# A transformer layer's output projection: a second of its seven block products split into seven small ones

## The chip, the cores and the metric

The kernel runs on one core of one Trainium2 chip. The metric is the device time of one execution in microseconds (us). A core has a matrix engine (TensorE, PE in the profile), three engines for elementwise work (VectorE, DVE; ScalarE, ACT; GpSimd, POOL), a queue engine (SyncE, SP) and 16 DMA engines. Each engine works through its own list of instructions in order and waits on semaphores. Transfers issued by SP and by POOL go through two queues to the same DMA engines; POOL's can add what they move to what lies at the destination.

## The reference

One layer on 512 tokens of width 2048, in float32:

```python
hn = rmsnorm(x, norm_g[i])
y = swa_mixer(hn, ...)            # windowed attention; ends with (out * silu(gate)) @ w_out
x = x + y
emb = p[i] @ ple_proj[i]
g = sigmoid(rmsnorm(x, ple_norm[i]) @ ple_gate[i])
x = x + emb * g
return rmsnorm(x, final_g)
```

The change concerns `(out * silu(gate)) @ w_out`, a product of 512x2048 with 2048x2048, and its addition to `x`.

## The kernel before

The kernel runs in stages: the first projections, attention with the gate's projection woven in (up to about 451 us of the span), the output projection (to about 600 us), the gate of the embeddings, the final norm. Every product keeps float32 accuracy from three matmuls (`mm3`, L124 to L126): each operand is split into a rounded high part and a low rest, and high x high, low x high and high x low are summed in PSUM. For the weights ACT rounds (`bhi`, L646) and DVE subtracts (`blo`, L647).

The output projection is cut into 2x2 blocks on both sides (tokens by channels, channels by outputs) and done by a scheme of Strassen's kind: seven block products instead of eight, of sums of blocks. The sums of activations (`Forms.steps`) are made by DVE; the sums of weights (`SUMS`) are made in DRAM during attention, by a copy on SP's queue and an accumulating transfer on POOL's. The products are numbered 1 to 7; product 1 is the negative one to which 6, 5 and 3 are added in the same PSUM banks.

A product has eight pieces, `(p, jj, m)`: `jj` is one of two halves of its 1024 outputs, `m` one of four parts of its 1024 channels, and each piece needs 512 KB of weights (128x1024) and makes 12 matmuls of 128x512. The list `OUT` sets the order of pieces, and for PE and SP with it the order of instructions; the other engines are ordered by a scheduler, except during attention, where the order is the written one on all engines. `Pieces` loads the weights three or four pieces ahead (`ahead`, `_prepare`) into three buffers of the tag `wraw` (`braw` in the profile) and splits them two or three ahead into three pairs `whi`, `wlo`. Between the pieces numbered `FOURTH` every fourth piece is split into a fourth pair, `spare`.

Product 4 is already made of seven small ones of the same scheme (class `Inside`), written "n" in `OUT`: 14 small pieces of 6 matmuls. Their weights stay in SBUF: product 6 loads its eight pieces into eight tiles `grown` ("seed"), and after use POOL adds another block to each of them (L703, accumulating from DRAM) and then forms the sums between tiles (L713, L723). The small pieces are woven between the pieces of product 3.

When the last piece of a half product is done, `add_y` adds it from PSUM to the one or two blocks of `x1` that need it (DVE, L1062 and L1064), or `add_in` for small products. `x1[j]` holds columns 512j to 512j+511 of x, four tiles of 128 tokens each, and is loaded from DRAM by `load_x`, four transfers of 1 MB on SP's queue, at the places `x_at`. ACT sums the squares for the next norm when a block is complete. The work of `later`, `extra` and `ahead` is given out piece by piece in the loop over `OUT`.

Of the kernel before, what the change touches and what calls it, by code (L numbers as in the profile page):

```python
# [20 lines left out]
P = 128  # L21
# [34 lines left out]
def trunk_kernel(ctx: ExitStack, tc: tile.TileContext, a: dict):  # L56
# [539 lines left out]

    SUMS = [("w_out", 7), ("w_out", 5), ("w_out", 6), ("ple_gate", 7), ("ple_gate", 5)]
    for nm, p in SUMS:
        for jj in range(2):
# [14 lines left out]
    class Pieces:  # L614
# [3 lines left out]
        def __init__(self):  # L618
            self.specs, self.base, self.made, self.grown, self.due = [], {}, {}, {}, []
            self.aside, self.first4, self.last4 = set(), 0, 0  # L620

# [3 lines left out]
        def _prepare(self, i):  # L625
# [62 lines left out]
    GROW = 4  # L688
    FOURTH = 24, 62
    FINAL_G = 6  # L690
# [3 lines left out]
    class Inside:  # L694
# [41 lines left out]
        def forms(self):  # L736
# [3 lines left out]
            for q in ORDER_IN:  # L740
# [17 lines left out]
                yield  # L758

    inside = Inside("w_out")  # L760
    SHARED = [(3, 0, 0), (3, 0, 1), "n", (3, 0, 2), "n", "n", (3, 0, 3), "n", (3, 1, 0), "n", "n", (3, 1, 1), "n", "n", (3, 1, 2), (3, 1, 3)]
    SHARED += ["n"] * (14 - SHARED.count("n"))
    OUT = [(p, jj, m) for p in (1, 7, 2, 6, 5) for jj in range(2) for m in range(4)] + SHARED

    def add_stage(nm, order):
        at = {}
        if nm == inside.nm:
            parts = [(q, i) for q in ORDER_IN for i in range(2)]
            for step in OUT:
                if step == "n":  # L770
                    B.add("part", inside, parts.pop(0))
                    continue
# [280 lines left out]
    def add_y(p, jj, tb, ps):  # L1053
# [5 lines left out]
        for (j, t), sign in whither:  # L1059
            xt = x1[j][:, t, :]  # L1060
            if sign > 0:
                nc.vector.tensor_add(xt, ps, xt)  # L1062
            else:
                nc.vector.tensor_sub(xt, xt, ps)  # L1064
            if p in (2, 5, 3, 4):
                squares(t, j)

    turns = []

# [19 lines left out]

    def inner_part():  # L1090

        x = None
        for q in ORDER_IN:
            if q in (1, 7, 2, 4):
                ps = bank(f"o4_{q}", {1: "t", 4: "t"}.get(q, "o"))
                x = ps if q == 1 else x
            else:
                ps = x
            for i in range(2):
                bh, bl = B.get(at)  # L1100
                fh, fl = inside.made[q]
                for kk in range(2):
                    k = 2 * i + kk
                    mm3(ps, fh[:, k], fl[:, k], bh[kk], bl[kk], q in (1, 7, 2, 4) and k == 0, k == 3, q in (6, 5, 3))
                if i == 1:
                    coming.append(partial_of(add_in, q, ps))
                yield

    def add_in(q, ps):
        whither = {  # L1110
# [3 lines left out]
        for (r, c), sign in whither:  # L1114
            j, t = c, 2 + r
            xt = x1[j][:, t, :]
# [7 lines left out]
    def turns_of(*v):  # L1124
        for kp, th, tag in v:
            turn(kp, th, tag)

    x_at = {(1, 1, 1): 0, (7, 0, 0): 2, (7, 0, 3): 1, (7, 1, 1): 3}
    waiting = {(7, 0): (1, 0), (2, 0): (1, 1)}
    held, coming = {}, []  # L1130
# [4 lines left out]
        (3, 0, 1): [partial_of(turn, 0, 0, "o")],  # L1135
        (3, 0, 3): [partial_of(turn, 1, 0, "o")],
        (3, 1, 0): [partial_of(turn, 2, 0, "o")],
        (3, 1, 1): [inner_forms, partial_of(turn, 3, 0, "o")], (3, 1, 2): [inner_forms], (3, 1, 3): [inner_forms],
        7: [partial_of(turn, 4, 0, "s")], 8: [partial_of(turn, 5, 0, "s"), ple_first],
# [3 lines left out]
    }  # L1143
    made, inner, seen = {}, inner_part(), 0
    ahead = {p: out_forms.steps(n) for p, n in zip((1, 7, 2, 6, 5), (7, 2, 6, 5, 3))}
    for at, step in enumerate(OUT):
        if step == "n":
            next(inner)
            step, p = seen, None
            seen += 1  # L1150
        else:
            p, jj, m = step
# [3 lines left out]
            next(made[p, jj], None)  # L1156
        for _ in range(-(-len(later) // 2)):
# [5 lines left out]
        if p in ahead:  # L1163
            next(ahead[p], None)
# [4 lines left out]
        if step == FINAL_G:  # L1169
            nc.sync.dma_start(fg, a["final_g"].partition_broadcast(P))  # L1170
    turns = []
    run(ple_first)
    assert not turns

# [295 lines left out]
```

## Time and profile before

| | |
|---|---|
| three runs | 795.31, 796.02, 797.12 us; median 796.02 |
| profiled execution | 795.63 us, its span 793.9 us |
| granted TensorE clock | 0.997 |
| DMA | 169.23 MB in the span, mean 213 GB/s |
| load of one piece, `braw<-in_w_out` | 512 KB, 4.7 us from issue to landing (median) |
| POOL's accumulating loads from w_out, 440 to 625 us | 8 of 512 KB, 11.3 us to landing (median) |

The span is measured from the first to the last instruction; the execution's own time is 1.7 us more. Busy times are summed per engine. An idle time is put down to what ended it. The DMA share is the mean busy share of the 16 DMA engines; it can read a little over 1 where packets overlap. A piece's number in the prediction is its place in `OUT`.

### The profile page before, as it was taken

What the parts mean: (1) busy time and instruction counts of PE and PEld (TensorE: products, weight loads), DVE (VectorE), ACT (ScalarE), POOL (GpSimd) and SP (SyncE); (2) the same over time, 40 slices, a digit from 0 to 9 for tenths busy, and PEclk for the clock granted to TensorE, in tenths of its full rate; (3) what the DMA queues carried; (4) which work ended last, traced back from release to release, by engine and by line L of the source; (5) the groups of instructions that cost most, each with busy time, mean ns of one, the idle gap of its engine ahead of it and who ended that gap; (6) DMA issues with size and microseconds to landing.
All of it is one profiled execution on the core that took longest, in us unless ns stands there. A gap on an engine that the chain in (4) does not pass through costs nothing.

```text
span 793.9 us, 11140 instructions
## 1 busy us (share of the span) xinstructions
PE 783.2 (99%) x3750; PEld 653.7 (82%) x3750; DVE 604.5 (76%) x1034; ACT 488.7 (62%) x999; POOL 156.9 (20%) x372
## 2 busy tenths in 40 slices
PE   9999999999999999999999999999999999999995
PEld 7888888888888888888888878888888888888884
DVE  4536478888877788687887889776888757899885
ACT  5632376677556766566666654654779756667754
POOL 0003013443243314333133200031100120200000
PEclk9999999999999999999999999999999999999998
DMA  8790585979677967889585569899973996885533
GB/s 337 275 221 8 189 239 164 249 212 252 184 224 194 228 192 201 210 225 263 151 222 130 150 217 355 330 254 303 272 218 99 358 222 218 166 217 194 170 107 106
DMA packets 45513, 169.23 MB, mean 213 GB/s; under 512 B 6464, under 2 KB 7104, under 8 KB 41616
## 3 DMA queue, kind: packets, MB, share of 16 engines
q1 hardware_dynamic: 36896, 129.01, 47.9%
q0 software_dynamic: 8272, 39.12, 26.2%
q8 instruction: 29, 0.48, 0.2%
q10 hardware_dynamic: 288, 0.39, 0.2%
q14 instruction: 28, 0.23, 0.1%
HBM read 157.44 MB, written 46.19 MB: 256 GB/s over the span
## 4 chain that ended last, share of the span: by engine, by line
PE 96%; DVE 2%; DMA 0%; issue 0%; ACT 0%; DVEq 0%
PE qps L124 7%; PE qps L126 7%; PE qps L125 7%; PE gps L124 7%; PE gps L125 7%; PE gps L126 7%; PE o L125 6%; PE o L126 6%; PE o L124 6%; PE g L126 6%; PE g L125 5%; PE g L124 5%; PE s L401 2%; PE vps L228 2%; PE o L523 2%; PE pt L479 2%
## 5 line engine op out<-in xcount | busy, mean ns | idle before, releaser
L646 ACT CAST bhi<-braw 128x1024 fp32r<-128x1024 f32 x75 | 78.9, 1052 | 62.4 <-PE g L126 18.2
L647 DVE TENSOR_TENSOR blo<-braw,bhi 128x1024 fp32r<-128x1024 f32 x75 | 91.8, 1226 | 28.4 <-ACT bhi L646 28.2
L124 PE MATMUL gps<-xh,whi 128*128 128x512 f32 x256 | 100.5, 393 | 0.0
L125 PE MATMUL gps<-xl,whi 128*128 128x512 f32 x256 | 100.0, 391 | 0.0
L126 PE MATMUL gps<-xh,wlo 128*128 128x512 f32 x256 | 99.9, 390 | 0.0
L503 POOL TENSOR_SCALAR_AFFINE_SELECT own<-r 64x256 fp32r<-64x256 f32 x96 | 60.8, 633 | 191.7 <-ACT r L484 109.3
L113 DVE TENSOR_TENSOR wlo<-wraw,whi 128x1024 fp32r<-128x1024 f32 x60 | 73.5, 1226 | 26.4 <-ACT whi L107 24.3
L124 PE MATMUL qps<-xh,whi 128*128 128x512 f32 x224 | 87.7, 392 | 0.0
L125 PE MATMUL qps<-xl,whi 128*128 128x512 f32 x224 | 87.4, 390 | 0.0
L126 PE MATMUL qps<-xh,wlo 128*128 128x512 f32 x224 | 87.4, 390 | 0.0
L461 ACT ACTIVATE t<-t,sm 128x129 f32<-128x129 f32 x128 | 50.6, 397 | 49.3 <-DVE sm L452 46.4
L124 PE MATMUL g<-bhi,fhg 128*128 128x512 f32 x192 | 75.2, 392 | 0.0
L126 PE MATMUL g<-bhi,flg 128*128 128x512 f32 x192 | 74.8, 390 | 0.0
L125 PE MATMUL g<-blo,fhg 128*128 128x512 f32 x192 | 74.7, 389 | 0.0
L107 ACT CAST whi<-wraw 128x1024 fp32r<-128x1024 f32 x60 | 62.1, 1037 | 16.8 <-DMA wraw<-in_w_q 16.8
L125 PE MATMUL o<-blo,fho 128*128 128x512 f32 x164 | 64.0, 391 | 0.1
L124 PE MATMUL o<-bhi,fho 128*128 128x512 f32 x164 | 64.0, 390 | 0.0
L126 PE MATMUL o<-bhi,flo 128*128 128x512 f32 x164 | 63.9, 390 | 0.0
L484 ACT CAST r<-pt 128x256 fp32r<-128x256 f32 x64 | 23.8, 372 | 55.6 <-PE pt L479 55.2
L126 PEld LDWEIGHTS gps<-xh,wlo 128*128 128x128 f32 x256 | 48.1, 188 | 10.6
L124 PEld LDWEIGHTS gps<-xh,whi 128*128 128x128 f32 x256 | 48.1, 188 | 9.0
L125 PEld LDWEIGHTS gps<-xl,whi 128*128 128x128 f32 x256 | 48.1, 188 | 8.8
(248 smaller groups left out, 1808.4 us busy)
## 6 DMA issues: line engine op xcount, KB each, us to landing
wraw<-in_w_gate_in SPq DMA_DIRECT2D x32, 512.0 KB, 5.0
wraw<-in_w_q SPq DMA_DIRECT2D x28, 512.0 KB, 5.9
w_out<-in_w_out POOLq DMA_DIRECT2D x24, 512.0 KB, 7.9
braw<-in_w_out SPq DMA_DIRECT2D x24, 512.0 KB, 4.7
braw<-in_ple_gate SPq DMA_DIRECT2D x24, 512.0 KB, 4.3
w_out<-in_w_out SPq DMA_DIRECT2D x16, 512.0 KB, 7.3
ple_gate<-in_ple_gate SPq DMA_DIRECT2D x16, 512.0 KB, 6.3
ple_gate<-in_ple_gate POOLq DMA_DIRECT2D x16, 512.0 KB, 5.9
```

The lines of the kernel that those rows point to most:

```text
L107: nc.scalar.copy(hi, self.raw[i])
L113: nc.vector.tensor_sub(lo, raw, hi.bitcast(F32))
L124: nc.tensor.matmul(ps, sh, mh, start=first, stop=False, skip_group_check=more)
L125: nc.tensor.matmul(ps, sh, ml, start=False, stop=False, skip_group_check=more)
L126: nc.tensor.matmul(ps, sl, mh, start=False, stop=last, skip_group_check=more)
L228: nc.tensor.matmul(v_ps[t], h[:, c], both[:, :, 256:512], start=f, stop=e, skip_group_check=True)
L401: nc.tensor.matmul(s_ps[:, u, : 2 * n], st, key[:, :, first : first + n], start=True, stop=True)
L461: nc.scalar.activation(su, su, AF.Exp, bias=sm[:, u : u + 1], accum_out=sm[:, 2 + u : 3 + u])
L484: nc.scalar.copy(r[:, 0], PT[i])
L503: nc.gpsimd.affine_select(out=cols(own[places[g % 2 ^ low]]), in_=cols(r[here, low].bitcast(F32)), pattern=[[sign * QB, 2], [0, GROUP], [s ...
L646: nc.scalar.copy(hi, raw)
L647: nc.vector.tensor_sub(lo, raw, hi.bitcast(F32))
```

## The change

Product 2 leaves the list of whole products and is made of seven small ones too, written "m" in `OUT`: 14 small pieces between the last pieces of product 7 and those of products 6 and 5. Their weights are loaded from DRAM, each small piece 512 KB, into two tiles of two places (`small`); four new sums of weights (`small_sum`) are made in DRAM during attention. Their activations (`small_forms`) use `fg`, `pTh` and `pTl`, which are free at that time. The blocks of x that the seventh product goes to (tiles 2 and 3 of each `x1[j]`) are no longer loaded first: ACT writes plus or minus the product into them (`nc.scalar.mul` in `add_y`), and POOL adds the rows of x with accumulating transfers (`add_x`, four of 512 KB). `load_x` loads the other two tiles, half as much. The fourth pair `spare` is used from piece 14 to 67, the sooner loading rules change in `ahead`, and in the first eight pieces of the stage all engines keep the written order.

```diff
+    def small_sum(q, first, more):
+        for i in range(2):
+            t = small[q, i] = tc.dram_tile([P, WE], F32, name=f"small_{q}_{i}")
+            copies.append((t, first(i)))
+            adds.append((t, more(i)))
+
+    small_sum(7, lambda i: small_piece(0, 1, i), lambda i: small_piece(1, 1, i))
...
+                elif kind == "small":
+                    n = small_place(key)
+                    if key in (0, 2):
+                        self.aside.append(rooms[0].tile([P, 2, WE], F32, tag="partial", name=f"small{key}", bufs=2))
+                    t = self.aside[n // 2][:, n % 2]
...
-                if n not in self.base and n >= self.done and kind not in ("grow", "part") and (kind == "seed" or n <= i + (4 if self.first4 <= i < self.last4 - 2 else 3)):
+                if n in self.base or n < self.done or kind in ("grow", "part"):
+                    continue
+                if kind == "one" and FIRST_SMALL <= n < LAST_SMALL:
+                    sooner = sum(self.specs[v][0] == "one" for v in self.base) < 3
+                else:
+                    sooner = kind == "seed" and n <= i + 6
...
-    FOURTH = 24, 62
+    FIRST_SMALL, LAST_SMALL = 14, 46
+
+    def small_place(key):
+        return key % 4 if key < 10 else 2 + key % 2
+
+    FOURTH = 14, 68
...
+    def small_forms(ahead):
+        v = lambda r, c: gates[2 + c][:, :, r * P : (r + 1) * P]
...
+            if sub:
+                nc.vector.tensor_sub(src, *sub)
+            fh, fl = (w[:, n % 2].rearrange("p (k t) -> p k t", k=4) for w in (pTh, pTl))
...
+                nc.scalar.copy(fh, src)
+                nc.vector.tensor_sub(fl, src, fh.bitcast(F32))
...
-    OUT = [(p, jj, m) for p in (1, 7, 2, 6, 5) for jj in range(2) for m in range(4)] + SHARED
+    OUT = [(p, jj, m) for p in (1, 7) for jj in range(2) for m in range(4)]
+    for n in (15, 14):
+        OUT.insert(n, "m")
+    for p, between in ((6, "01111011"), (5, "11101110")):
+        for n in range(8):
+            OUT.append((p, n // 4, n % 4))
+            if between[n] == "1":
+                OUT.append("m")
+    OUT += SHARED
...
-        nc.sync.dma_start(x1[j], a["x"].rearrange("(t p) d -> p t d", p=P)[:, :, j * 512 : (j + 1) * 512])
+        nc.sync.dma_start(x1[j][:, :2], a["x"].rearrange("(t p) d -> p t d", p=P)[:, :2, j * 512 : (j + 1) * 512])
+
+    def add_x(j):
+        nc.gpsimd.dma_start(
+            x1[j][:, 2:], a["x"].rearrange("(t p) d -> p t d", p=P)[:, 2:, j * 512 : (j + 1) * 512], accum_op=ALU.add
+        )
...
-            if sign > 0:
+            if p == 7:
+                nc.scalar.mul(xt, ps, float(sign))
+            elif sign > 0:
                 nc.vector.tensor_add(xt, ps, xt)
...
-    x_at = {(1, 1, 1): 0, (7, 0, 0): 2, (7, 0, 3): 1, (7, 1, 1): 3}
-    waiting = {(7, 0): (1, 0), (2, 0): (1, 1)}
+    x_at = {(1, 1, 2): 0, (7, 0, 2): 1, (6, 1, 1): 2, (6, 1, 3): 3}
+    waiting = {(7, 0): (1, 0), (6, 0): (1, 1)}
```

The order of the loads on SP's queue, from the last piece of product 7 on. `braw` are loads into the three buffers, `grown` those of product 6, `small` those of the small products. Before:

```order
L635 DMA braw_5234<-w_out_1_3_753 128x1024
L635 DMA braw_5254<-in_w_out 128x1024
L1018 DMA x_3_4965<-in_x 128x4x512
L635 DMA braw_5275<-in_w_out 128x1024
L635 DMA braw_5293<-in_w_out 128x1024
L635 DMA braw_5313<-in_w_out 128x1024
```

In the change:

```order
L657 DMA braw_5244<-w_out_1_3_753 128x1024
L657 DMA small_5311<-small_0_746 128x1024
L657 DMA grown_5327<-w_out_0_2_772 128x1024
L657 DMA small_5311<-small_1_747 128x1024
L657 DMA grown_5357<-w_out_0_3_773 128x1024
L657 DMA small_5173<-small_0_758 128x1024
L657 DMA grown_5400<-w_out_1_0_774 128x1024
L657 DMA small_5173<-small_1_759 128x1024
L657 DMA grown_5436<-w_out_1_1_775 128x1024
L657 DMA grown_5458<-w_out_1_2_776 128x1024
```

Where product 2 was loaded through the three buffers, small pieces and the tiles of product 6 now alternate, each with a place of its own.

POOL's accumulating transfers in the stage. Before, the first are those to the `grown` tiles:

```order
L703 DMA grown_5434<-in_w_out 128x1024
L703 DMA grown_5361<-in_w_out 128x1024
L703 DMA grown_5386<-in_w_out 128x1024
L703 DMA grown_5409<-in_w_out 128x1024
L703 DMA grown_5459<-in_w_out 128x1024
```

In the change:

```order
L1096 DMA x_2_4988<-in_x 128x2x512
L1096 DMA x_0_4986<-in_x 128x2x512
L740 DMA grown_5036<-in_w_out 128x1024
L740 DMA grown_5082<-in_w_out 128x1024
L1096 DMA x_3_4989<-in_x 128x2x512
L1096 DMA x_1_4987<-in_x 128x2x512
L740 DMA grown_5327<-in_w_out 128x1024
```

Four additions to x stand ahead of and between the eight to the `grown` tiles, twelve where there were eight.

DVE's list around product 5's first pieces (in the old program split for four whole pieces). `blo` and `spare` are the splits of weights. Before:

```order
L845 TENSOR_TENSOR flo_00_5705<-gate_3977,fho_00_5704 128x512
L647 TENSOR_TENSOR blo_5606<-braw_5581,bhi_5605 128x1024
L845 TENSOR_TENSOR flo_01_5728<-gate_3977,fho_01_5727 128x512
L647 TENSOR_TENSOR blo_5630<-braw_5603,bhi_5629 128x1024
L845 TENSOR_TENSOR flo_10_5771<-gate_4564,fho_10_5770 128x512
L647 TENSOR_TENSOR blo_5649<-braw_5627,bhi_5648 128x1024
```

In the change:

```order
L669 TENSOR_TENSOR blo_5617<-braw_5567,bhi_5616 128x1024
L817 TENSOR_TENSOR pTl<-gate_4587,pTh 128x512
L669 TENSOR_TENSOR spare<-small_5173,spare 128x1024
L1198 TENSOR_TENSOR x_0_4986<-o_2_5583,x_0_4986 128x512
L907 TENSOR_TENSOR gate_4587<-gate_4587,gate_2862 128x4x256
L669 TENSOR_TENSOR blo_5651<-braw_5596,bhi_5650 128x1024
L669 TENSOR_TENSOR blo_5665<-small_5311,bhi_5664 128x1024
L920 TENSOR_TENSOR flo_10_5845<-gate_4587,fho_10_5844 128x512
```

Between two splits for whole pieces now stands one for a small piece, with the small products' forms and additions.

More of the change, by code (lines that the diff above doesn't have):

```diff
@@ L768, in add_stage @@
             parts = [(q, i) for q in ORDER_IN for i in range(2)]
+            smalls = [(q, i) for q in ORDER_IN for i in range(2)]
             for step in OUT:
+                if step == "m":
+                    q, i = smalls.pop(0)
+                    raw = {1: (0, 0), 2: (1, 0), 3: (1, 1)}.get(q)
+                    B.add("small", small_piece(*raw, i) if raw else small[q, i], 2 * ORDER_IN.index(q) + i)
+                    continue
                 if step == "n":
@@ L1143, in trunk_kernel @@
     }
-    made, inner, seen = {}, inner_part(), 0
-    ahead = {p: out_forms.steps(n) for p, n in zip((1, 7, 2, 6, 5), (7, 2, 6, 5, 3))}
+    extra[7, 0, 2] = extra[7, 1, 0] = [smalls]
+    extra[6, 0, 0] = [partial_of(add_x, 0), partial_of(add_x, 1)]
+    extra[6, 0, 1] = [partial_of(add_x, 2), partial_of(add_x, 3)]
+    order = ExitStack()
+    order.enter_context(
+        tc.manual_schedule(
+            engines={getattr(mybir.EngineType, v) for v in ("PE", "SP", "Pool", "DVE", "Activation")}
+        )
+    )
+    made, inner, seen = {}, inner_part(4, inside.made, {1: "t", 4: "t", 7: "o", 2: "o"}), 0
+    inner2, seen2 = inner_part(2, small_made, {1: "t", 7: "t", 2: "o", 4: "o"}), 0
+    ahead = {p: out_forms.steps(n) for p, n in zip((1, 7, 6, 5), (7, 6, 5, 3))}
     for at, step in enumerate(OUT):
+        if at == 8:
+            order.close()
         if step == "n":
@@ L1150, in trunk_kernel @@
             seen += 1
+        elif step == "m":
+            next(inner2)
+            step, p = ("m", seen2), None
+            seen2 += 1
+            if seen2 % 2 == 0:
+                next(smalls, None)
         else:
@@ L1156, in trunk_kernel @@
             next(made[p, jj], None)
-        for _ in range(-(-len(later) // 2)):
+        for _ in range(len(later) if step in (8, 9) else -(-len(later) // 2)):
             later.pop(0)()
```

59 lines of the change are left out of this document (45 added, 14 removed).

## The prediction

> **What bounds the kernel now.** I read the page's head first, then who waits for whom on TensorE (PE), then the stages in a table of windows, and last the transfers in windows of one to fifteen microseconds. The head and the waits of PE over the whole execution:
>
> ```profile
> span 793.9 us, 11140 instructions
> PE 783.2 (99%) x3750; PEld 653.7 (82%) x3750; DVE 604.5 (76%) x1034; ACT 488.7 (62%) x999; POOL 156.9 (20%) x372
> PE warm_ps L145 <- PEq L1460: 0.8, 1, 0.8
> PE qps L216 <- ACT xh L199: 0.4, 1, 0.4
> ```
>
> PE is busy 99% of the span and waits 1.2 us in all, at its first two steps. So only fewer matmuls shorten this kernel, and each new wait of PE lengthens it. In the stage that is changed (columns of the windows: stretch, length, busy time of PE, its weight loads, DVE, ACT and POOL with counts, clock, DMA share, GB/s):
>
> ```profile
> 470.00:500.00 30.00, 30.00 (x134) 24.59 (x133) 26.12 (x31) 14.79 (x18) 0.00 (x0) 1.00 0.84 310
> 500.00:530.00 30.00, 30.00 (x134) 24.86 (x133) 22.70 (x27) 17.16 (x24) 6.14 (x7) 1.00 0.99 320
> 530.00:560.00 30.00, 30.00 (x134) 24.85 (x133) 19.73 (x22) 13.92 (x19) 4.58 (x6) 1.00 1.04 286
> ```
>
> PE has no gap, but look at the last two columns: the DMA engines are as good as always busy from 500 to 560. They are the resource with nothing left, and the change asks more of them.
>
> **What is removed: 12 matmuls.** A whole product is 96 matmuls of 128x512; seven small ones are 7 x 12 = 84. One must not be priced at its row's 0.39 us, since they overlap; the price is the distance between starts (timeline of PE: the stage's first matmul, then the first and last of seven in a row):
>
> ```profile
> 451.73 0.40 PE L124 MATMUL o<-bhi,fho 128*128 128x512 f32 x1
> ...
> 470.12 0.39 PE L125 MATMUL o<-blo,fho 128*128 128x512 f32 x1
> ...
> 471.48 0.39 PE L125 MATMUL o<-blo,fho 128*128 128x512 f32 x1
> ```
>
> Six steps in 1.36 us are 0.227 each; 12 x 0.227 = **2.7 us gained**. A large piece (12 matmuls) thus takes 2.72 us, a small one (6) 1.36 us. I number the stage's pieces from 0 in the new order: piece n starts at 451.7 plus the pieces before it.
>
> Two small stalls at the stage's start can go too:
>
> ```profile
> 460.42 0.50 PE L125 MATMUL o<-blo,fho 128*128 128x512 f32 x1
> 474.18 0.19 PEld L125 LDWEIGHTS o<-blo,fho 128*128 128x128 f32 x1 [0.25 <-DVE blo L647]
> ```
>
> The first comes from DVE doing two 128x1024 differences before the third split; the new order puts one of them later, so this 0.25 us should go. I count **0.3 us** for the two.
>
> **What is added on DVE and ACT.** Prices are again distances between starts:
>
> ```profile
> 474.05 0.68 DVE L1064 TENSOR_TENSOR x<-x,o 128x512 f32<-128x512 f32 x1
> 474.64 0.69 DVE L845 TENSOR_TENSOR flo<-gate,fho 128x512 fp32r<-128x512 f32 x1
> 475.25 1.22 DVE L647 TENSOR_TENSOR blo<-braw,bhi 128x1024 fp32r<-128x1024 f32 x1
> 476.38 1.22 DVE L832 TENSOR_TENSOR gate<-gate,gate 128x1024 f32<-128x1024 f32 x1
> 453.34 0.61 ACT L844 CAST fho<-gate 128x512 fp32r<-128x512 f32 x1
> 453.86 0.59 ACT L571 ACTIVATE gps<-gate 128x512 f32<-128x512 f32 x1
> ```
>
> On DVE 0.60 us for 128x512, 1.14 for 128x1024; on ACT 0.52 for 128x512 (from 453.34 to 453.86). Six more splits cost DVE 6.8 us; the forms of the small products are 7 splits and 4 differences where product 2 had 4 splits (7 x 0.60 = 4.2 more); 8 small additions to x replace 4 of product 2 (2.4 more); the seventh product's 8 additions leave DVE (4.8 less) and become 8 writes on ACT (4.2 us, and ACT is half idle from 470 to 500). DVE gains 8.6 us of work over 150 us. The thickest place is pieces 24 to 38: in the new order 16 DVE operations of 1024 and 17 of 512 stand there, 18.2 + 10.2 = 28.4 us, and PE takes 8 x 2.72 + 7 x 1.36 = 31.3 us over them. So DVE is 91% full and still fits. I cost it at **nothing**; the cover is PE's own work, and without it (see the rivals) it would be some 3 us. Eight more sums of weights in DRAM, 16 transfers, run during attention, where PE has not waited for a weight once; nothing, and at worst the 16.8 us that ACT idles there for weights grows by a fifth, still off PE.
>
> ```profile
> L107 ACT CAST whi<-wraw 128x1024 fp32r<-128x1024 f32 x60 | 62.1, 1037 | 16.8 <-DMA wraw<-in_w_q 16.8
> ```
>
> **What is added on the transfers.** This decides. Only loads were under way from 505 to 520, only accumulating transfers of POOL (q0) from 520 to 535:
>
> ```profile
> DMA packets 1585, 5.80 MB, mean 387 GB/s; under 512 B 175, under 2 KB 175, under 8 KB 1581
> q1 hardware_dynamic: 1581, 5.76, 98.4%
> DMA packets 903, 3.31 MB, mean 220 GB/s; under 512 B 97, under 2 KB 97, under 8 KB 902
> q0 software_dynamic: 809, 2.99, 100.6%
> ```
>
> Both fill the engines, at 387 and 220 GB/s. So a load of 512 KB (0.524 MB) costs 1.36 us of all engines, an accumulating one 2.38. In the new order the stage loads a piece for every small matmul group as well: pieces 20 to 45 are 26 loads in 57 us, and 8 additions to the grown tiles and the 4 new ones to x fall into the same stretch. From 475 to 555 (what must be there for piece 46) I count, before, 34 units of loads (28 pieces, three loads of x of two units each), 8 accumulating and then two copies and two accumulating ones of the sums: 46.2 + 10 x 2.38 + 2 x 1.36 = 72.7 us of 80. After: 34 loads again (31 pieces and three half loads of x) but 12 accumulating, and the same four of the sums: 46.2 + 14 x 2.38 + 2.7 = 82.2 us of 80. The stretch is overbooked, by 2 us on paper.
>
> What that costs PE depends on who is served. When they were issued before, and after (timeline of POOL):
>
> ```profile
> 516.14 1.80 POOL L703 DMA_DIRECT2D grown<-in_w_out  x2 [65.96 <-DMA grown<-w_out]
> 531.33 0.88 POOL L703 DMA_DIRECT2D grown<-in_w_out  x1 [1.84 <-DVE spare L647]
> 541.81 0.56 POOL L713 DMA_DIRECT2D sum<-grown  x1 [9.60 <-issue]
> 560.30 0.86 POOL L723 DMA_DIRECT2D grown<-grown  x1 [3.78 <-DMA sum<-grown]
> ```
>
> In the old program the 8 additions fell on product 6, whose weights already lay in SBUF, and the loads paused. In the new one the first addition to x waits only for ACT's writes of the seventh product's first half: that half ends at 451.7 + 12 x 2.72 = 484.3, the four writes end near 487, and the first bytes of an accumulating transfer came some 4 us after issue (516.14; the first software packets are those of 520 to 521, below), so 491. From there they queue up: the writes and splits release twelve from 487 to about 519, one every 2.7 us, and each takes 2.4 or more. With both kinds queued, the windows of one microsecond from 517, from 520 (software packets begin) and from 540 (both rows), then the loads' row from 538 and that from 539 to 542:
>
> ```profile
> q1 hardware_dynamic: 108, 0.40, 102.3%
> q0 software_dynamic: 24, 0.10, 52.8%
> q0 software_dynamic: 36, 0.14, 71.6%
> q1 hardware_dynamic: 34, 0.14, 36.7%
> q1 hardware_dynamic: 39, 0.16, 41.5%
> q1 hardware_dynamic: 111, 0.39, 34.7%
> ```
>
> From 517 two accumulating transfers were already issued and had moved nothing. From 540 both move, and each gets the same 0.14 MB per us: 3.74 us for one load instead of 1.36. [...]
>
> Now the walk. SP's queue is held up at the load of piece 17, whose buffer comes free with the split of piece 12, near 481.4. Behind it nine loads stand free, into buffers of their own. At 1.36 us each, after what is still queued, loads up to piece 23 have landed at 491. The next twelve are pieces 24 to 33, a half load of x, and piece 34: 12 x 3.74 = 45 us, so piece 34's weights land at 536. It starts on PE at 532.1 and needs them 2.5 us earlier (a cast of 1.05, a subtraction of 1.22, two handovers): 529.6. PE would wait **6.3 us** there. At 0.16 MB per us (from 538) it is 12 x 3.28 and a wait of 0.8; at 0.13 (0.39 MB in 3 us from 539) it is 12 x 4.03 and 9.8. Below: nothing, if loads go first as at 517; POOL's last two additions can wait, as their sums begin late. I take 5.5 us, a bit under the equal share, because the additions stop for a moment between splits.
>
> Sum: -2.7 - 0.3 + 5.5 = **+2.5 us**. On the profiled execution (795.63, that is the span of 793.9 and 1.7 around it) this is 798.1; the median of the runs is 796.02, so I predict **798.5 us**. Times within 0.2% (1.6 us) of before count as the same, which is about what a measurement of this kernel can tell.
>
> **The rivals.** (1) *The loads win.* It needs little: they must move 0.163 instead of 0.14 MB per us for the twelve to land in 38.5 us, and at 517 they took everything. Many loads queue at once here, where at 540 there were two or three. Then the wait is 0 to 1.4 us and the time 796.0 - 3.0 + 0 to 1.4 = 793.0 to 794.4. It decides from a share of about 0.16 on. (2) *Something between, or DVE.* A wait of 1.4 to 4.6 us gives 794.4 to 797.6. DVE alone can make it:
>
> ```profile
> DVE blo L647 <- ACT bhi L646: 15.1, 20, 2.2
> ```
>
> It waited 15.1 us for ACT in the 160 us from 450, 9%; 9% of pieces 24 to 38 is 2.8 us, against 2.9 of room and a lead of three pieces. So hardly more than 1 us. (3) *Worse:* the sums of the fourth product's weights, which follow from about 540, keep half of the engines while pieces 38 to 46 still need a load every 2.1 us. A load that met such traffic took
>
> ```profile
> braw<-w_out SPq DMA_DIRECT2D x1, 512.0 KB, 7.7
> ```
>
> (issued at 534). Five more us of waiting give 803 to 806. Against it: a PE that waits lets the transfers catch up.
>
> **How the numbers follow.** The forecast (wait of 4.6 to 10 us, time 797.6 to 803.0) gets 0.41, rival (1) 0.36, (2) 0.12, (3) 0.11. So faster 0.36, the same 0.12, slower 0.52. The range from 793.0 to 803.0 leaves out (3) and a few hundredths below; the forecast's own range is 797.6 to 803.0.
>
> **What would show it.** Right: PE or its weight loads wait on DVE's blo, and ACT's casts on transfers, between 525 and 560, 4 to 10 us in all; the software queue is busy without a pause from 491 to about 535; the loads of pieces 30 to 38 take 10 us and more to land; PE's count is 12 lower. Wrong: PE runs through without a gap (rival 1), and the span is 791; or PE waits for a blo whose cast was done long before (DVE); or the wait lies after 560, at the sums.

## The result, and the profile after

The change makes the kernel slower: 806.0 us (median of four runs, 804.83 to 806.73) against 796.3 us of the kernel before on the same chip. The ratio is 1.0121, with a 95% interval of 1.0101 to 1.0140. The forecast was 798.5 us, its range ended at 803.0: right in the sign, too small by 7.5 us. The profiled execution has a span of 805.0 us, 11.1 more than before. The head of the page, and who waited for whom on PE from 440 to 640 us (in total, times, longest):

```profile
span 805.0 us, 11199 instructions
PE 785.0 (98%) x3738; PEld 653.1 (81%) x3738; DVE 612.4 (76%) x1043; ACT 499.6 (62%) x1016; POOL 169.8 (21%) x384
```

```profile
PE o L124 <- ACT bhi L668: 7.2, 1, 7.2
PE o L125 <- DVE blo L669: 2.3, 4, 0.7
```

The 12 matmuls are gone (3738 for 3750), and in their place PE has waits that the kernel before did not have. Most of it is one wait, 7.2 of 9.5 us. Its place in the windows (stretch, length, busy time of PE, weight loads, DVE, ACT, POOL, then granted clock, DMA share, GB/s) and in PE's timeline:

```profile
520.00:530.00 10.00, 10.00 (x45) 8.08 (x45) 6.32 (x8) 4.20 (x5) 0.86 (x1) 1.00 1.07 268
530.00:540.00 10.00, 3.57 (x15) 2.28 (x13) 2.42 (x3) 1.05 (x1) 0.00 (x0) 0.80 1.06 270
540.00:550.00 10.00, 7.58 (x23) 5.44 (x24) 6.79 (x7) 6.54 (x9) 1.10 (x2) 0.69 1.03 367
```

```profile
533.91 0.39 PE L126 MATMUL o<-bhi,pTl 128*128 128x512 f32 x1
541.51 0.80 PE L124 MATMUL o<-bhi,fho 128*128 128x512 f32 x1 [7.21 <-ACT bhi L668]
542.77 0.80 PE L125 MATMUL o<-blo,fho 128*128 128x512 f32 x1 [0.46 <-DVE blo L669]
543.37 0.63 PE L126 MATMUL o<-bhi,flo 128*128 128x512 f32 x1
543.79 0.63 PE L124 MATMUL o<-bhi,fho 128*128 128x512 f32 x1
...
546.27 0.40 PE L124 MATMUL o<-bhi,fho 128*128 128x512 f32 x1
546.50 0.40 PE L125 MATMUL o<-blo,fho 128*128 128x512 f32 x1
```

From 533.91 to 541.51 PE stands before piece 34, the piece that the prediction named. Read on: the next matmuls do not start 0.23 us apart but 0.42 (543.37 to 543.79), and only from 546.27 on 0.23 again, and the granted clock falls to 0.69 in that window. The wait is followed by a second, smaller loss. What PE waited for is two steps back, in ACT's timeline and in that of SP, whose transfer it was:

```profile
540.41 1.04 ACT L668 CAST bhi<-braw 128x1024 fp32r<-128x1024 f32 x1 [8.85 <-DMA braw<-w_out]
```

```profile
511.97 0.32 SPq L657 DMA_DIRECT2D braw<-w_out  x1
```

The load of piece 34 was issued at 511.97 and had landed at 540.4: 28.4 us for 512 KB. By the prediction's price its bytes keep the engines 1.36 us, and in the kernel before a load of this size landed after 4.7 us (median).

The 11.1 us of the span: the first output matmul starts 0.9 us later (452.66 for 451.73; the runs below that are built on the change start there between 451.60 and 452.45, so I take this for the spread of executions), the stage from there to the first matmul of the next takes 166.2 instead of 155.8 us, the rest 0.2 less. In the stage I add up every distance between two matmuls beyond 0.227 us: 13.3 us from 529 to 573, 11 of waits (7.4 before piece 34, the others about 1 us or less each, from 529 to 573) and some 2 of slow steps behind it. Then 13.3 - 2.7 - 0.4 (the old small stalls) = 10.2, beside the 10.4 measured.

### The profile page after: what moved, and what is told of

It reads as the page before. It is cut to its first block, busy times and chain, and to the rows that moved or that the text cites. A ratio compares the mean times of both kernels' runs of the same rounds, so it can differ in the third digit from the quotient of the medians.

```text
span 805.0 us, 11199 instructions
## 1 busy us (share of the span) xinstructions
PE 785.0 (98%) x3738; PEld 653.1 (81%) x3738; DVE 612.4 (76%) x1043; ACT 499.6 (62%) x1016; POOL 169.8 (21%) x384
## 4 chain that ended last, share of the span: by engine, by line
PE 85%; DMA 7%; DVE 4%; issue 1%; ACT 1%; SPq 0%; DVEq 0%; ACTq 0%
PE qps L124 7%; PE qps L126 7%; PE qps L125 7%; PE gps L124 7%; PE gps L125 7%; PE gps L126 7%; PE g L126 5%; PE g L125 5%; PE g L124 5%; DMA small<-small 4%; PE o L125 3%; DMA grown<-w_out 3%; PE o L126 3%; PE o L124 3%; PE s L401 2%; PE o L523 2%
## 5 line engine op out<-in xcount | busy, mean ns | idle before, releaser
L669 DVE TENSOR_TENSOR blo<-braw,bhi 128x1024 fp32r<-128x1024 f32 x68 | 83.3, 1225 | 32.9 <-ACT bhi L668 32.5
L668 ACT CAST bhi<-braw 128x1024 fp32r<-128x1024 f32 x68 | 71.5, 1053 | 58.9 <-DMA braw<-w_out 16.7
L124 PE MATMUL o<-bhi,fho 128*128 128x512 f32 x132 | 52.4, 397 | 7.2 <-ACT bhi L668 7.2
L126 PEld LDWEIGHTS gps<-xh,wlo 128*128 128x128 f32 x256 | 48.1, 188 | 10.6
L125 PE MATMUL o<-blo,fho 128*128 128x512 f32 x132 | 52.7, 400 | 1.6 <-DVE blo L669 1.6
L126 PE MATMUL o<-bhi,flo 128*128 128x512 f32 x132 | 52.0, 394 | 0.0
```

The source lines that it names most:

```text
L124: nc.tensor.matmul(ps, sh, mh, start=first, stop=False, skip_group_check=more)
L125: nc.tensor.matmul(ps, sh, ml, start=False, stop=False, skip_group_check=more)
L126: nc.tensor.matmul(ps, sl, mh, start=False, stop=last, skip_group_check=more)
L668: nc.scalar.copy(hi, raw)
L669: nc.vector.tensor_sub(lo, raw, hi.bitcast(F32))
```

## The experiments

Twelve runs, each a kernel beside the kernel before on the same chip. In the column "against the change" the difference of the two ratios is multiplied by 796 us; by the two intervals each such difference is uncertain by some 2 us. The "theory of turns" of the expectations is the guess that the two queues move packet for packet while both have work. The counts agree with it in the prediction's microsecond from 540 of the kernel before (36 and 34 packets) and from 510 to 530 in the change (943 and 943).

| run | what differs | median us | ratio to before (95%) | against the change |
|---|---|---|---|---|
| the change | | 806.0 | 1.0121 (1.0101 to 1.0140) | |
| seventh_on_dve | the small products alone | 801.4 | 1.0059 (1.0041 to 1.0077) | -4.9 |
| seventh_alone | the seventh product's new way alone | 801.2 | 1.0058 (1.0042 to 1.0073) | -5.0 |
| no_add_x | no transfers that add x | 795.5 | 0.9986 (0.9972 to 1.0000) | -10.7 |
| plain_x | they overwrite instead of adding | 801.6 | 1.0074 (1.0057 to 1.0091) | -3.7 |
| long_rows | they have rows of 4 KB | 806.2 | 1.0129 (1.0113 to 1.0146) | +0.6 |
| six_loads_less | six weight loads fewer | 793.8 | 0.9972 (0.9956 to 0.9988) | -11.9 |
| x_loads_later | two half loads of x later | 802.5 | 1.0072 (1.0057 to 1.0087) | -3.9 |
| fill_wait | idle PE filled with matmuls | 804.4 | 1.0096 (1.0078 to 1.0114) | -2.0 |
| adds_late | additions of x after 550 | 806.3 | 1.0129 (1.0113 to 1.0145) | +0.6 |
| adds_loads_late | and two half loads later | 807.5 | 1.0145 (1.0130 to 1.0160) | +1.9 |
| adds_split | additions late and cut in two | 797.3 | 1.0009 (0.9998 to 1.0019) | -8.9 |
| adds_split_mid | and two half loads later | 799.7 | 1.0052 (1.0033 to 1.0071) | -5.5 |

**Which part costs?** First each half of the change by itself. seventh_on_dve keeps the small products and undoes the rest: x is loaded whole at the old places and DVE adds the seventh product.

```diff
-        nc.sync.dma_start(x1[j][:, :2], ...[:, :2, j * 512 : (j + 1) * 512])
+        nc.sync.dma_start(x1[j], ...[:, :, j * 512 : (j + 1) * 512])
...
-            if p == 7:
-                nc.scalar.mul(xt, ps, float(sign))
-            elif sign > 0:
+            if sign > 0:
...
```

> Product 2 stays in small pieces; the seventh product is added by DVE again and x is loaded whole by SP at the places it had before (four loads of 1 MB early in the stage). Theory of turns: the software queue has only the eight additions to the grown tiles; the loads of x run before them, while the load queue is alone, but push the early loads of pieces back by some 3 us; PE waits 0 to 4 us, time 793 to 798. Rival (bytes): 2.1 MB move from 220 to 387 GB/s, 4 us less transfer time, 800 to 803. Rival (DVE): eight more additions of 0.6 us on a list that is 91% full between pieces 24 and 38, so it gets slower than the change, 807 to 811.

seventh_alone is the kernel before with the other half: ACT writes the seventh product, x is loaded by half, and POOL adds the rest.

```diff
...
-            if sign > 0:
+            if p == 7:
+                nc.scalar.mul(xt, ps, float(sign))
+            elif sign > 0:
...
+    extra[2, 0, 2] = [partial_of(add_x, j) for j in range(4)]
```

> The kernel before with the other part of the change alone: product 2 whole, the seventh product written by ACT, half loads of x and the four additions of x rows. Theory of turns: the additions meet product 2's loads, which need 128 packets per 2.72 us, 47 per us, against some 44 to 50 that their turn gives; they are late by little, and product 6 behind them has no three buffers to wait for: 796 to 799. Rival (bytes): the stretch had room for 9.5 us more transfer time, 796. Rival (DVE): 4.8 us less on DVE, 796 or a bit less.

Each half alone costs about 4.7 us, and together they cost 9.6: the two add up. seventh_on_dve fell in the range of the rival that counts bytes; seventh_alone missed all three of its expectations, which ended at 799. seventh_alone has the clearer lesson, since it removes no matmul and adds no load. It swaps 2 MB of plain loads (four half loads) for 2 MB of accumulating transfers. PE's waits in it, 440 to 640 us:

```profile
PE o L125 <- DVE blo L647: 2.7, 5, 0.8
PE o L124 <- ACT bhi L646: 1.4, 2, 0.9
PE o L125 <- DVE spare L647: 0.4, 1, 0.4
```

By the prediction's own prices this swap books 4 x (2.38 - 1.36) = 4.1 us more time of the engines, and 4.5 us of waits came. No room took it up in this order of loads. In seventh_on_dve PE waits at another place, first for 2.0 us at 487.5, because a cast by ACT stood 4.2 us for its weights (ACT's timeline); x is loaded whole and earlier there, and the loads of weights come behind it.

```profile
483.87 1.05 ACT L668 CAST bhi<-braw 128x1024 fp32r<-128x1024 f32 x1 [4.15 <-DMA braw<-w_out]
```

So this wait too begins with a transfer, and is not the work of the additions that DVE has again: the first of them starts at 487.37. But some 1.3 of the 2.0 us are DVE's. The cast was done at 484.92, and the split that PE waited for came only behind two operations on activations in DVE's list (DVE's timeline):

```profile
486.23 1.22 DVE L669 TENSOR_TENSOR blo<-braw,bhi 128x1024 fp32r<-128x1024 f32 x1
```

**Engine time, or turns of the queues?** no_add_x leaves the four transfers out (x is then missing in those rows).

```diff
-    extra[6, 0, 0] = [partial_of(add_x, 0), partial_of(add_x, 1)]
-    extra[6, 0, 1] = [partial_of(add_x, 2), partial_of(add_x, 3)]
```

> The four additions of x rows by POOL's accumulating transfers are left out (tokens 256 to 511 lose x itself); all else as in the change. Theory of turns: the software queue loses 1024 of its 2048 packets, the loads have the engines nearly alone until about 497 and after about 525; PE's wait at piece 34 is gone and the time is 793 to 795 us, the gain of 2.7 us or a little less. Rival (bytes): 2.1 MB fewer at 220 GB/s are 9.5 us of transfer time, so 796 to 798. Rival (DVE and ACT): their lists are the same, 804 to 806.

```profile
PE o L125 <- DVE blo L669: 1.3, 3, 0.7
PE o L125 <- DVE spare L669: 0.7, 1, 0.7
```

PE's waits shrink from 9.5 to 2.0 us and the time falls by 10.7, to 795.5 us. That lies between the ranges of the two theories (793 to 795, and 796 to 798) and decides neither. It is 2.7 us for each of four transfers, where the prediction had 2.38; but in this run the granted clock stays at 1.00 (every window from 440 to 620), so some 2 us of the 10.7 are the slow steps that are gone. And this run gains hardly more than 1 us on the kernel before, so the weights of the small products have already used up most of what the 12 matmuls gave.

Two runs then change what the four transfers are, not where: plain_x lets them overwrite, long_rows gives them half as many packets of twice the size.

```diff
 # plain_x
-            x1[j][:, 2:], ...[:, 2:, j * 512 : (j + 1) * 512], accum_op=ALU.add
+            x1[j][:, 2:], ...[:, 2:, j * 512 : (j + 1) * 512]
 # long_rows
-            x1[j][:, 2:], ...[:, 2:, j * 512 : (j + 1) * 512], accum_op=ALU.add
+            x1[j][:, 2:].rearrange("p t c -> p (t c)"), block("w_out", 1, 1, 0, j), accum_op=ALU.add
```

> The change, but the four transfers of POOL's queue to rows 256 to 511 of x overwrite what is there instead of adding to it (left out of the computation: the seventh product in these rows). Same queue, same place, same packets. Theory A (the DMA engines are full from 495 to 570, and what counts is how long each transfer keeps them: an accumulating one 2.38 us, a plain one 1.36): 4 x 1.02 us less, 806.0 - 4.1, so 801 to 803. Theory B (the two queues take turns by packet, and the 2 KB rows of x cost the loads as many turns whatever is done with them): 805 to 807.

> The change, but the four accumulating transfers take a block of w_out with rows of 4 KB instead of the rows of x of 2 KB (left out of the computation: x in rows 256 to 511, w_out stands there instead). Same bytes, half the packets. Theory A (engine time by bytes and by whether it accumulates): no change, 805 to 807. Theory B (turns by packet): the four take half as many turns from the loads, and the loads behind them come some 5 us earlier, 799 to 802.

Both came out as theory A said: 801.6 (801 to 803 expected) and 806.2 (805 to 807). Overwriting saves 0.94 us a transfer, for the 1.02 worked out from the rows of before; half as many packets for the same bytes made no difference to the time (+0.6 us). (They changed the course: in long_rows no wait of PE is above 1.1 us, and eleven shorter ones stand in place of the long one.) The queues' rows from 510 to 530 us show why turns are not the price. First the change, then long_rows (packets, MB, share of the 16 engines):

```profile
q0 software_dynamic: 943, 2.49, 64.3%
q1 hardware_dynamic: 943, 3.10, 42.1%
```

```profile
q0 software_dynamic: 748, 2.74, 68.5%
q1 hardware_dynamic: 749, 2.73, 36.5%
```

The counts are equal in both runs (943 and 943, 748 and 749). But with the rows of 2 KB more packets pass in the 20 us, 1886 for 1497, and nearly the same bytes, 5.59 MB for 5.47: the engines' time is full in both (the shares sum to 106% and 105%).

**Is it only the accumulating transfers?** six_loads_less removes plain loads instead.

```diff
-                nc.sync.dma_start(t.rearrange("p (k c) -> p k c", k=2) if kind == "proj" else t, src)
+                if kind != "small" or key not in range(4, 10):
+                    nc.sync.dma_start(t.rearrange("p (k c) -> p k c", k=2) if kind == "proj" else t, src)
```

> The change, but six of the fourteen weight pieces of the small products (those of the third, fourth and fifth of them) are not loaded; what lies in the buffer is used again (left out of the computation: the right weights in these three small products). Theory A (what counts is the engines' time booked in this stretch, whichever queue it is on): 6 x 1.5 us less, of which all but the last of the waits can be had: 797 to 799.5. Rival (the loads fit beside the others, and only the accumulating transfers hold PE up): 803 to 807.

```profile
PE o L125 <- DVE spare L670: 0.3, 1, 0.3
PE o L125 <- DVE blo L670: 0.2, 1, 0.2
```

793.8 us, below the expected 797: the waits of PE are gone but for 0.5 us, and the slow steps with them (the clock is 1.00 in every window from 440 to 620). So plain loads on SP's queue hold PE up too, and not the accumulating transfers alone. This run still has all that the change adds on DVE, on ACT and to the sums in DRAM. That it is 2.2 us faster than before (0.28%, interval 0.12% to 0.44%), next to the 3.0 that the prediction took off for matmuls and small stalls, shows that these cost almost nothing.

It shows one thing more. This run and seventh_alone move the same in the stage, on both queues (452 to 606 us, first seventh_alone, then six_loads_less):

```profile
q1 hardware_dynamic: 7858, 27.27, 48.8%
q0 software_dynamic: 3680, 11.54, 38.4%
```

```profile
q1 hardware_dynamic: 7866, 27.31, 48.6%
q0 software_dynamic: 3680, 11.54, 37.6%
```

Yet the one has 4.5 us of waits and the other 0.5, and their ratios lie 6.8 us apart, where matmuls and small stalls make 3.0. Some 4 us therefore hang on something else than the amount of traffic. The order of the transfers and the buffers that they wait for are the plain difference between the two, but no run tests them alone.

x_loads_later only moves two transfers, of 1 MB together, behind the worst place:

```diff
-    x_at = {(1, 1, 2): 0, (7, 0, 2): 1, (6, 1, 1): 2, (6, 1, 3): 3}
+    x_at = {(1, 1, 2): 0, (7, 0, 2): 1, (5, 1, 3): 2, (3, 0, 1): 3}
```

> The two half loads of x that stand in SP's queue ahead of pieces 34 and 37 are moved behind the loads of piece 46. Theory (the two queues take turns packet by packet, and a row of x is a packet of 2 KB where a row of weights is 4 KB): the half load ahead of piece 34 is 256 packets, and at the 44 packets per us that the load queue got from 525 to 530 that is 5.8 us. So PE's wait at piece 34 falls from 7.4 to 1 to 2 us, the clock does not drop, and the time is 796 to 799 us. Rival (there are simply too many bytes in the stretch, whatever their order): the bytes are the same, 804 to 806. Rival (DVE and ACT are late with splits): nothing is changed for them, 806.

It gained 3.9 us, between the two expectations, where the two loads book 2 x 1.36 = 2.7. PE's wait before piece 34 fell to 1.1 us, as the theory said, but waits of about 1 us now stand before pieces 34 to 36, and the clock drops all the same (0.66 from 540 to 550, last section).

**The slow steps behind the wait.** fill_wait puts 30 matmuls that nobody reads ahead of piece 34.

```diff
+        if at == 34:
+            fill_ps, fh = bank("fill", "t"), out_forms.made[5][0][0]
+            for _ in range(30):
+                nc.tensor.matmul(fill_ps, fh[:, 0, :P], fh.rearrange("p k t -> p (k t)"), start=True, stop=True)
```

> The change, with 30 matmuls of 128x512 into a bank that nobody reads ahead of piece 34 on PE (nothing is left out); at 0.227 us each they take 6.8 us, which is less than PE waits there. Theory: the weights of piece 34 come at the same time, but PE no longer stands still before it, so its twelve matmuls run at 0.23 us instead of 0.43: 2.2 us less, 803 to 804.5. Rival: the slower steps behind the wait come from something else than the idle PE (the clock was lowered for that stretch anyway, or the matmuls are fed slowly): no change, 805.5 to 807.

804.4 us, as expected of the theory, and the windows show the clock (fill_wait):

```profile
530.00:540.00 10.00, 9.47 (x42) 7.51 (x40) 2.51 (x5) 1.57 (x2) 0.00 (x0) 1.00 1.06 276
540.00:550.00 10.00, 7.92 (x32) 5.93 (x33) 7.19 (x10) 6.26 (x9) 1.09 (x2) 1.00 1.03 376
```

1.00 in both windows, where the change has 0.80 and 0.69. The load of piece 34 is no quicker (issued at 509.09, its cast starts at 537.74: 28.7 us, for 28.4 in the change), but behind it the steps are 0.23 us apart and not 0.42. So the idle PE cost more than its wait here: some 2 us by the slow steps of the change's trace. The ratios give 2.0 as well, but their intervals overlap, and in the profiled execution that load was also issued 2.9 us sooner than in the change, so they do not show the clock alone.

**Can the transfers be put where there is room?** The windows of no_add_x from 560 on (the DMA share is the last number but one):

```profile
560.00:570.00 10.00, 9.30 (x43) 7.31 (x42) 8.05 (x11) 6.87 (x12) 0.85 (x1) 1.00 0.78 220
570.00:580.00 10.00, 10.00 (x48) 8.27 (x47) 9.56 (x11) 8.50 (x14) 0.86 (x1) 1.00 0.82 243
580.00:600.00 20.00, 20.00 (x99) 16.52 (x98) 16.58 (x20) 15.85 (x29) 1.74 (x2) 1.00 0.61 166
```

Some 12 us of the engines are free there. adds_late moves the four additions into that stretch, with the squares of the second half of the columns behind them.

```diff
...
-    extra[6, 0, 0] = [partial_of(add_x, 0), partial_of(add_x, 1)]
-    extra[6, 0, 1] = [partial_of(add_x, 2), partial_of(add_x, 3)]
+    extra[3, 0, 0].append(partial_of(add_x, 2))
+    extra[3, 0, 2] = [partial_of(add_x, 3)]
+    extra[4].append(partial_of(add_x, 1))
+    extra[6].append(partial_of(add_x, 0))
+    for j in (2, 3):
+        extra[8 + j - 2] += [partial_of(squares, t, j) for t in (2, 3)]
```

> The change, with the four accumulating transfers to x moved from product 6 to product 3 and the four squares of columns 1024 to 2047 of rows 256 to 511 moved behind them; everything else stays. Theory A (the stretch from 495 to 560 is overbooked, from 560 to 600 the engines have some 12 us free in the run without the transfers): they cost nothing there, 794.5 to 797.5. Rival: they meet the sums of product 4's weights and hold the last loads up, so that PE's wait only moves behind 560: 799 to 804.

> As adds_late, and the two half loads of x for columns 1024 to 2047 also moved to the end of product 5. Theory A: another 2.7 us of the engines leave the overbooked stretch, and the run without the transfers had 3.4 us of waits left there, so 792.5 to 795.5, faster than before. Rival: the half loads only move the wait, 796 to 801.

Both missed: 806.3 and 807.5, with nothing gained. From 520 to 560 the waits of PE were indeed down to under 2 us, but adds_late has a new one (all waits, 560 to 620 us):

```profile
DVE x L1198 <- DMA x<-in_x: 10.6, 1, 10.6
...
PE o L125 <- DVE spare L669: 7.5, 3, 6.2
```

The last transfer into x was still on its way when DVE had to add a small product to the same block. DVE stood 10.6 us, every split behind it in its list stood too, and PE waited 6.2 us for one of them. The rival had the right place for the wait, behind 560, but not its cause. In adds_loads_late PE also waits 2.9 us at 583, behind a cast by ACT that stood for a sum of product 4's weights, now sharing the engines with the late half loads and the additions (DMA share 1.06 from 570 to 580; ACT's timeline):

```profile
581.42 1.04 ACT L668 CAST bhi<-grown 128x1024 fp32r<-128x1024 f32 x1 [6.48 <-DMA grown<-sum]
```


adds_split therefore cuts the additions to the first half of the columns into single blocks of 128 rows, each in a gap between DVE's additions to that block:

```diff
...
-    extra[4].append(partial_of(add_x, 1))
-    extra[6].append(partial_of(add_x, 0))
+    extra[3, 0, 3] += [partial_of(add_x, 0, 2, 3), partial_of(add_x, 1, 2, 3)]
+    extra[4].append(partial_of(add_x, 1, 3, 4))
+    extra[6].append(partial_of(add_x, 0, 3, 4))
```

> As adds_late, but the transfers to columns 0 to 1023 are cut into their two blocks of 128 rows, each issued in a gap between two additions by DVE to the same block. Theory A (the transfers cost nothing once they lie behind 560 and no addition of DVE stands right behind them): 795 to 798. Rival (the engines are not free enough behind 560 either, and the sums or the last loads come late): 800 to 805.

```profile
PE o L125 <- DVE blo L669: 2.3, 4, 0.8
PE tp L1121 <- ACT hT L1128: 0.5, 1, 0.5
PE g L125 <- DVE blo L669: 0.5, 2, 0.3
PE o L125 <- DVE spare L669: 0.3, 1, 0.3
```

The waits are those of PE from 440 us on. 797.3 us: the same rows of x, added by the same kind of transfer (six of them now), cost 8.9 us less, and the kernel is level with the one before (0.9998 to 1.0019). No wait is longer than 0.8 us. adds_split_mid tried to take the last of it by also moving the two half loads of x into product 5.

```diff
-    x_at = {(1, 1, 2): 0, (7, 0, 2): 1, (6, 1, 1): 2, (6, 1, 3): 3}
+    x_at = {(1, 1, 2): 0, (7, 0, 2): 1, (5, 0, 1): 2, (5, 1, 0): 3}
```

> As adds_split, but the half loads of x for columns 1024 to 2047 are issued two thirds of the way through the small products (in product 5) instead of in product 6. Theory A: adds_split still waits 1.8 us around 535 and 1.7 us around 560; the two half loads kept the engines for 2.7 us ahead of both, and ahead of the first only after this edit, so 1 to 2 us less than adds_split: 795 to 796.5, at the time of before. Rival: the half loads only push the wait to 558 or to the sums of product 4's weights behind it: 797 to 799.

A miss: 799.7 us. The waits near 535 went, but one of 1.9 us at 561 came (PE's waits in it):

```profile
PE o L124 <- ACT bhi L668: 1.9, 1, 1.9
```

and its six runs spread from 798.4 to 803.2. No complete version beat the kernel before.

## Why the prediction was right or wrong

**The matmuls and the small stalls** were right: 12 fewer, and no wait between 452 and 529 us.

**DVE, ACT and the sums in DRAM at nothing** were right for the change, shown by six_loads_less. The rival in which DVE makes the wait falls with it. In seventh_on_dve, where DVE has the additions as well, its order did add to a wait.

**The mechanism** was right: piece 34, its cast on a transfer (8.85 us), loads that take 10 us and more (28.4), and the software queue at work throughout (61.4% of the engines from 491 to 540, below).

**The step that failed is the walk that gave 5.5 us of waiting**; measured are 13.3. Three things are in the difference.

First, the backlog. The walk had "loads up to piece 23 have landed at 491", and then twelve loads up to piece 34. It had the load of piece 17 free near 481.4. DVE's split that freed its buffer came later, and SP issued it only behind that split (DVE's and SP's timelines):

```profile
483.26 1.22 DVE L669 TENSOR_TENSOR blo<-braw,bhi 128x1024 fp32r<-128x1024 f32 x1
```

```profile
484.50 0.33 SPq L657 DMA_DIRECT2D braw<-w_out  x1
```

It took 6.9 us to land, so that at 491 the loads had come to piece 17 and not to piece 23. The loads' rows from 481 to 491, and both queues' from 491 to 540:

```profile
q1 hardware_dynamic: 941, 2.94, 82.4%
```

```profile
q0 software_dynamic: 2113, 5.84, 61.4%
q1 hardware_dynamic: 2401, 8.27, 45.0%
```

From 481 to 491 the loads moved 2.94 MB, 5.6 loads of 0.524 MB, where 1.36 us each makes 7.4. And from 491 to the landing of piece 34 they moved 8.27 MB, 15.8 loads and not twelve: pieces 20 to 34 and the half load of x are 16 (18 and 19 had been loaded before). The share itself was better than assumed: 8.27 MB in 49 us is 0.169 MB per us, above the 0.14 of the forecast, which carried the row of one microsecond over the whole stretch as an estimate, and even above the 0.163 from which rival (1) was to win. The two queues moved equally many packets from 510 to 530 (943 and 943); what the loads had of that in bytes went with the size of the packets. With the additions' rows of 2 KB the loads moved 3.10 MB in the 20 us from 510, with the rows of 4 KB in long_rows 2.73: the share was larger beside the short packets. So the share was under-estimated, the queue more so, and piece 34 landed at 540.4 instead of 536: 7.4 us there for the 6.3 of the walk, cut to 5.5.

Second, the other pieces. The walk followed one load; every piece up to 573 us came out of the same queue, and further waits, each about 1 us or less, add 3.7 us.

Third, the clock: some 2 us of slow steps, of which the prediction had no term. In the change's trace a step takes 0.42 us instead of 0.23 after PE had been idle for 7.2 us, and the windows from 537 to 545 show a granted clock of 0.50; in fill_wait, where PE is kept busy, the clock is 1.00.

Two readings of the prediction were off besides. The 2.38 us of an accumulating transfer come from a row of 3.31 MB that holds 0.31 MB of the loads; by the software queue's own row (2.99 MB in 100.6% of 15 us) it is 2.6, and by the loads' own row (5.76 MB in 98.4%) a load is 1.34. And pieces 20 to 45 take 54 us, not 57; nothing was built on that.

**What would have come nearer** is the count that the prediction made and then set aside. It found 82.2 us of transfers for 80 us and called the stretch overbooked by 2 us, as if the 7.3 us between 72.7 and 80 had been free before. The kernel before had less: its DMA share from 475 to 500 is 0.90, and from 500 to 555 it is 1.01, so that some 2.5 us were free. With so little free time, most of the added engine time is a loss. Priced by the prediction's rows for the whole stage, in us:

| edit | booked | measured |
|---|---|---|
| small products: 14 small loads for 8, less the matmuls | 6 x 1.36 - 2.7 = +5.5 | +4.7 |
| the seventh product's transfers | 4 x (2.38 - 1.36) = +4.1 | +4.6 |
| both, less the small stalls | +9.3 | +9.6 |
| the change without the four additions | -4 x 2.38 = -9.5 | -10.7 |
| the four plain instead of accumulating | -4.1 | -3.7 |
| six loads fewer | -6 x 1.36 = -8.2 | -11.9 |
| two half loads later | -2.7 | -3.9 |

The first three are against the kernel before, the others against the change. All but one fall within 1.2 us of the booking. This sum was made after the runs, and some of the fit is luck: the measured +9.6 holds some 2 us of slow steps that no booking has, and so does the -10.7. In six_loads_less 1.7 us remain over even without them. Against the kernel before it books +4.1 - 3.0 = +1.1 and is 2.2 us faster. So the sum gives the size of the loss, and what decides the rest, the order of the loads most likely, stays open. The prediction had counted the same number of loads, 34, before and after, because it looked at 475 to 555 us alone; over the whole stage SP issues six loads of weights more.

**Rival (3)** named the sums of product 4's weights as the place of the further loss. The long wait was ahead of them; behind 560 the change lost only 1.5 us, and whether the sums or the backlog made these was not told apart. But adds_loads_late shows that traffic beside those sums can be paid for (2.9 us of PE's waiting at 583).

## What to carry to other kernels

Where the DMA engines are at 1.0 over a stretch and the compute engine has no gap, count a transfer that is added there at its engine time, on whichever queue it is issued, and add up the booked time before following single loads. Here the edits cost or gained 0.85 to 1.45 times their booking; two kernels with the same traffic in the stage, in another order, differed by some 4 us, so the sum is a first size and no law. An accumulating transfer keeps the engines 1.75 to 2 times as long as a plain one here (2.38 and 1.36 us for 512 KB by the prediction's prices, 2.6 and 1.34 by the queues' own rows), so a store that saves a load but needs an addition later is no saving in such a stretch. Work moved to a place where the engines are free must also stand clear of the instruction that next touches the same block, or that instruction waits for the landing and so does the work behind it in its engine's list: in adds_late DVE stood 10.6 us, and PE 6.2 us for a split behind it.

## What the runs showed of the hardware that was not expected

The clock fell without a long pause too. In x_loads_later no single wait of PE from 440 to 640 is above 1.2 us, and still matmuls from 543 on last 0.63 us for 0.39 and the window shows a clock of 0.66 (PE's timeline and the window of that run):

```profile
533.48 0.50 PE L124 MATMUL o<-bhi,fho 128*128 128x512 f32 x1 [1.10 <-ACT bhi L668]
534.74 0.50 PE L125 MATMUL o<-blo,fho 128*128 128x512 f32 x1 [0.76 <-DVE blo L669]
...
538.59 0.50 PE L125 MATMUL o<-spare,pTh 128*128 128x512 f32 x1 [0.76 <-DVE spare L669]
539.16 0.40 PE L124 MATMUL o<-spare,pTh 128*128 128x512 f32 x1
541.13 0.79 PE L124 MATMUL o<-bhi,fho 128*128 128x512 f32 x1 [1.11 <-ACT bhi L668]
542.39 0.79 PE L125 MATMUL o<-blo,fho 128*128 128x512 f32 x1 [0.47 <-DVE blo L669]
543.40 0.63 PE L124 MATMUL o<-bhi,fho 128*128 128x512 f32 x1
```

```profile
540.00:550.00 10.00, 8.42 (x24) 6.34 (x24) 6.53 (x8) 6.64 (x9) 1.99 (x3) 0.66 1.03 369
```

The waits ahead of the slow matmuls were short, 0.76 us at 538.6 and 1.11 us at 541.1. Two of the same length a piece earlier (1.10 and 0.76 us at 533 to 535) had not lowered the clock (1.00 from 530 to 540), and in seventh_alone five waits of 0.5 to 0.9 us between 513 and 524 left it at 1.00 (both windows from 510 to 530), so what decides was not settled. In x_loads_later the late loads cost more than their lateness though no wait looks long: eleven steps from 542.98 to 547.67 take 0.43 us instead of 0.23, some 2.2 us together.
